# Expert products of a mixture-of-experts layer: float32 weights as the stationary operand, 21 load slots, h2 in natural column order

## The chip, the cores and the metric

The kernel runs on one core of a Trainium2 chip, in one launch. The core has TensorE (PE), VectorE (DVE), ScalarE (ACT), GpSimd (POOL) and SyncE (SP), each with its own queue of instructions, and DMA queues that are filled by SP and POOL. The metric is the device time of a launch in microseconds, lower is better.

## What is computed

One layer of a decoder for 1024 tokens of 1024 channels, all in float32: a modulated RMS norm, forgetting attention (8 heads) beside causal pooling, an output projection with residual, then a second modulated norm and a mixture of 32 small gated MLPs of which each token takes two, and a last norm. What the change touches is the second half:

```python
h = modulate(rmsnorm(x, norm_ffn_g), sh_f, sc_f)               # called h2 in the kernel
lg = h @ w_rg + b_rg                                           # 4 groups: the best one, with its probability
le_sel = (h @ w_re + b_re)[chosen group]                       # 8 experts of the group: the best two, softmax
for g in range(4):
    a = einsum('td,edf->tef', h, w_gate[g])                    # 1024 -> 256 per expert
    b = einsum('td,edf->tef', h, w_up[g])
    act = silu(a) * b * comb[:, g, :, None]                    # comb is 0 for the experts not chosen
    y = y + einsum('tef,efd->td', act, w_down[g])              # 256 -> 1024
x = rmsnorm(x + gt_f * y, norm_final_g)
```

## The kernel before

The work is tiled by 128 tokens (eight tiles) up to the router, and by expert behind it. Most of SBUF is one tile, `arena`, in which views are placed by hand at kB offsets.

**The order.** The instructions of PE, ACT, DVE and POOL are issued in the order in which the program writes them. Up to the first experts that order is `ORDER` (from line 38), a list of tokens: `om` and `oe` are the output projection of a tile and its residual, `xg` (`x1g`, line 898) multiplies x1 by the norm's factor into h2, `na` (`norm_ops`, 903) ends the norm and stores h2 with a DMA, `ro`, `rm` and `rt` transpose h2, multiply it with the router and choose, `po`, `pq` count positions, `tb` (line 1164) writes the table of each expert's tokens, `cp`, `ct`, `pc` the table of weights, `ld` is a load by SP.

**An expert.** `ex_gather` (1057) is a DMA on POOL's queue that fetches the rows of up to CAP = 100 tokens of an expert from h2 in DRAM; `ex_xt` (1080) transposes them on PE, eight transposes, and ACT and DVE copy them out of PSUM as two f16 halves. `load_chunks` (675 to 688) loads the weights, three chunks of 1 MB for an expert (gate, up, down) into the next of 14 slots of 8 kB per partition (`SLOTS`, 113); from expert 8 on a POOL memset of one element of the slot stands ahead of a load (`gate`). Since the products are made of f16 numbers, each chunk is split first: a high half (`ex_split`, by ACT, line 190 or 236) and the rest (DVE, 191, or POOL, 238). `mm3` (203 to 205) then multiplies high by high, high by low and low by high: in `ex_gu` X is the stationary operand (100 columns) and gate and up side by side are the moving one (512 columns). `ex_act` makes silu(gate) times up, `ex_at` (1103) transposes that, `ex_down` multiplies it with down, `ex_y` (1126) weighs it and `ex_scatter` (1118) adds it to x1 in DRAM by a DMA.

The experts 0 to 2 are begun in `ORDER`; the loop behind it interleaves an expert's gate and up with the down product of the one before, the transposes of the next, the splits of the next and the loads. The last two experts are kept apart and added to rows that were gathered before; `fin_load` and `fin_all` (1276 to 1304) are the last norm.

**h2's columns.** h2 is written in another column order (column 8p + j of a row lands at 128j + p), so that transposing contiguous pieces gives X in the order in which a weight chunk lies, eight rows of it in a partition. So `x1g` and `fin` (908) read and write with a stride.

Of the kernel before, what the change touches and what calls it, by code (L numbers as in the profile page):

```python
# [22 lines left out]
P = 128  # L23
S = 1024
D = 1024
# [11 lines left out]
GATE = 8  # L37
# [54 lines left out]
ld.6 oe51 pq40 av371 rt46 om600 pq41 xg51 av372 oq51 av373 bl7 om601 ho37 cm6 na50 ld.7 cm7 ld.8  # L92
ld.9 ce6 ld.10 na51 ce7 ro50 na52 ro51 na53 na54 na55 om602 om603 rm5 oe60 rt50 oq60 rt51 rt52 xg60
rt53 xs0001 rt54 xs0011 om610 om611 om612 rt55 om613 oe61 xg61 oq61 xs0101 om700 po5 na60 rt56 na61
na62 pq50 na63 pq51 om701 na64 om702 ro60 ro61 om703 om710 rm6 xs0111 na65 rt60 oe70 oq70 xg70 rt61
rt62 rt63 rt64 rt65 om711 om712 om713 oe71 xs0201 rt66 xm1 oq71 xg71 na70 po6 pq60 pq61 na71 gt na72
xm0 na73 na74 xs1001 ld.11 ro70 ro71 na75 xm2 ld.12 rm7 rt70 rt71 rt72 rt73 rt74 rt75 rt76 po7 pq70
pq71 tb cp xn0 xn1 xn2 xs0210 pc xs1100 ct ld.13 ld.14 xt00 ld.15 ld.16 xt01 xn3 xt10 xt11 gu00 xn4
gu01 xs1011 ld.17 ac0 xs1110 xs1200 xs1211 ld.18 ld.19 gu10 at0 xt20 xt21 xn5 xs2000 gu11 dw00 dw01
xs2100 ey0 sc0 xs2011 xs2110 ac1 xs2200 xs2210 ld.20 ld.21 ld.22  # L100
# [12 lines left out]
SLOTS = (40, 24, 96, 64, 72, 80, 88, 104, 0, 8, 16, 32, 56, 48)  # L113
# [4 lines left out]
def build(nc, tc, io, dbg=None):  # L118
# [559 lines left out]
    def load_chunks(upto, gate=False):  # L678
# [169 lines left out]
    wr_l = cview([P, KD, 36], F16)  # L848
    tl = {}
# [38 lines left out]
    def pj(ap, n):  # L888
        return ap.rearrange("t (p j) -> t p j", p=P)[:, n * 64:(n + 1) * 64]

    def jp(ap, n):
        return ap.rearrange("t (j p) -> t p j", p=P)[:, n * 64:(n + 1) * 64]

    def x1g(i, n):
# [27 lines left out]
    def route_t(i, q):  # L922
        h2 = tl[i]["h2"]
        hT(lambda j: h2[:, j * P:(j + 1) * P], q)
# [6 lines left out]

    def route_bias():
        sv = shf_b.rearrange("t (p j) -> t j p", p=P)
        for q in range(2):
            hT(lambda j: sv[:, j], q)
        pr = logit_mm()
        nc.vector.scalar_tensor_tensor(br_b, pr[:, 0:36], IWS, br_b, op0=OP.mult, op1=OP.add)
# [89 lines left out]
    def comb_table(o, r, dst):  # L1027
        pt = table(o, r.rearrange("p a b c -> p a (b c)"))
        nc.vector.tensor_reduce(dst, pt[:, 0:3 * NE].rearrange("p (a b) -> p b a", b=NE), axis=AX.X, op=OP.add)
        nc.vector.tensor_scalar(dst, dst, IWS / 4096.0, None, op0=OP.mult)  # L1030

    def b2_first():
# [3 lines left out]
        for g in range(4):  # L1036
            nc.sync.dma_start(wr_r[:, :, g * 8:(g + 1) * 8],
                              io["w_router_expert"][0, g].rearrange("(p j) e -> p j e", p=P))
        nc.sync.dma_start(wr_r[:, :, NE:], io["w_router_group"][0].rearrange("(p j) e -> p j e", p=P))
        load_chunks(1)  # L1040

    r_gh = Ring((152, 128), [KD, 2 * DE], F16)
    r_gl = Ring((144, 136), [KD, 2 * DE], F16)
    r_dnh = Ring((120, 160), [2, D], F16)
    r_dnl = Ring((124, 164), [2, D], F16)
    r_X = Ring((112, 116, 188), [D])
# [385 lines left out]
```

## Time and profile before

| | |
|---|---|
| Median of 3 runs | 909.32 us (907.1 to 912.29) |
| Span of the profiled execution | 909.4 us |
| PE busy | 734.2 us, 81% |
| DVE busy | 706.2 us, 78% |
| ACT busy | 499.5 us, 55% |
| POOL busy | 425.3 us, 47% |
| Moved by the DMA engines | 200.73 MB, mean 221 GB/s |

The shares are means over very different stages: the attention and pooling half runs to some 460 us, the router's end to 507 us, the experts to 871 us, the last norm to the end. A group of rows gives, for a line of the program, the busy time and what ended the idle time ahead of it; the rows of the timeline give single stretches. A matmul's record holds a fixed part that overlaps with the next one, so the price of one in a row of equals is the distance between their starts.

### The profile page before, as it was taken

Reading aid. Unit: us, or ns where it says so; the run is one execution under the profiler, and the core shown is the slowest. Engines: PE = TensorE matmul, PEld = TensorE weight load, DVE = VectorE, ACT = ScalarE, POOL = GpSimd, SP = SyncE. Lnnn points to the kernel's source line nnn. Section 1 sums busy time; section 2 is a strip of 40 time slices with the busy share of each in tenths; the row PEclk is TensorE's granted clock in tenths of the full one; section 3 lists DMA queues with packets and bytes.
Section 4 is the critical chain, followed back from the end, with each engine's and each line's share of the span. In section 5 each row is a group of like instructions: output and inputs, shape, how many; then the busy total and the mean of one; then the engine's idle time right before and its main releaser. Section 6 shows DMA issues by size and latency. Waiting matters only on the chain. (4 is left out here: it accounts for less than half of the span.)

```text
span 909.4 us, 13948 instructions
## 1 busy us (share of the span) xinstructions
PE 734.2 (81%) x4891; PEld 436.0 (48%) x4892; DVE 706.2 (78%) x1407; ACT 499.5 (55%) x776; POOL 425.3 (47%) x320
## 2 busy tenths in 40 slices
PE   2699999997978999889884299999887787888920
PEld 1358575343446565566642255555544454444510
DVE  4949877998785879967599569999877777777963
ACT  4455323221256354467744188898766677667750
POOL 2422501242104355367724357787756666565830
PEclk9999999998998999999997599999989899899975
DMA  8946675455875131125285669998999999999373
GB/s 288 383 167 202 199 230 144 135 160 160 223 215 163 62 114 37 71 106 174 83 328 204 196 205 309 354 327 291 328 309 307 302 321 320 309 317 303 79 281 124
DMA packets 108867, 200.73 MB, mean 221 GB/s; under 512 B 26219, under 2 KB 79075, under 8 KB 100598
## 3 DMA queue, kind: packets, MB, share of 16 engines
q1 hardware_dynamic: 97030, 181.83, 59.1%
q0 software_dynamic: 11760, 17.94, 8.5%
q8 instruction: 40, 0.66, 0.3%
q14 instruction: 37, 0.30, 0.1%
HBM read 177.27 MB, written 32.05 MB: 230 GB/s over the span
## 5 line engine op out<-in xcount | busy, mean ns | idle before, releaser
L191 DVE SCALAR_TENSOR_TENSOR arena<-arena 128x1024 f16<-128x1024 f32 (+1 forms) x168 | 215.5, 1306 | 44.6 <-ACT arena L190 39.1
L190 ACT ACTIVATE arena<-arena 128x1024 f16<-128x1024 f32 (+1 forms) x168 | 169.5, 1057 | 51.5 <-DMA arena<-in_w_expert_down 23.0
L205 PEld LDWEIGHTS <-arena 128*128 128x128 f16 (+1 forms) x912 | 100.8, 112 | 113.3 <-issue 26.7
L203 PEld LDWEIGHTS <-arena 128*128 128x128 f16 (+1 forms) x912 | 101.7, 113 | 102.0 <-ACT arena L1105 23.3
L204 PEld LDWEIGHTS <-arena 128*128 128x128 f16 (+1 forms) x912 | 101.4, 113 | 80.7 <-issue 19.6
L1118 POOL DMA_INDIRECT x_d<-arena,toki x30 | 102.0, 3399 | 78.9 <-DVE arena L1126 68.7
L238 POOL TENSOR_TENSOR arena<-arena 128x1024 f16<-128x1024 f32 x40 | 95.6, 2389 | 72.2 <-ACT arena L237 71.3
L786 POOL TENSOR_TENSOR arena<-arena 128x512 f16<-128x512 f32 (+1 forms) x72 | 83.2, 1165 | 70.2 <-ACT arena L785 34.8
L204 PE MATMUL pg<-arena 128*100 128x512 f16 x256 | 98.2, 383 | 4.4 <-DVE arena L191 4.3
L203 PE MATMUL pg<-arena 128*100 128x512 f16 x256 | 98.7, 386 | 1.3 <-ACT arena L190 1.3
L205 PE MATMUL pg<-arena 128*100 128x512 f16 x256 | 97.8, 382 | 0.0
L784 ACT ACTIVATE arena<-pst,psh_c 128x512 f32<-128x512 f32 (+1 forms) x80 | 52.4, 655 | 49.2 <-PE pst L777 24.1
L203 PE MATMUL py<-arena 128*100 128x512 f16 x128 | 53.8, 421 | 20.5 <-ACT arena L1105 20.5
L530 DVE SCALAR_TENSOR_TENSOR arena<-arena,cact 128x256 f32<-128x256 f32 x112 | 65.3, 583 | 2.4
L203 PE MATMUL pp<-arena 128*128 128x512 f16 x160 | 62.2, 389 | 4.6 <-DVE arena L654 4.6
L1057 POOL DMA_INDIRECT arena<-h_d,toki x32 | 55.6, 1738 | 16.6 <-PE pxt L1080 9.2
L204 PE MATMUL pp<-arena 128*128 128x512 f16 x160 | 62.0, 387 | 0.1
L205 PE MATMUL pp<-arena 128*128 128x512 f16 x160 | 61.9, 387 | 0.0
L208 ACT ACTIVATE arena<-arena 128x1024 f16<-128x1024 f32 (+2 forms) x34 | 29.1, 856 | 55.7 <-POOL arena L878 28.6
L622 POOL TENSOR_TENSOR arena<-arena 128x1039 f32<-128x1039 f32 (+3 forms) x10 | 22.7, 2266 | 79.1 <-issue 53.9
L205 PE MATMUL py<-arena 128*100 128x512 f16 x128 | 54.1, 423 | 1.0 <-DVE arena L1106 1.0
L731 DVE TENSOR_REDUCE mx<-psn 128x1 f32<-128x512 f32 (+3 forms) x76 | 47.1, 653 | 9.4 <-PE psn L730 7.6
(264 smaller groups left out, 1762.0 us busy)
## 6 DMA issues: line engine op xcount, KB each, us to landing
arena<-in_w_expert_gate SPq DMA_DIRECT2D x32, 1024.0 KB
arena<-in_w_expert_up SPq DMA_DIRECT2D x32, 1024.0 KB
arena<-in_w_expert_down SPq DMA_DIRECT2D x32, 1024.0 KB
arena<-in_w_ada SPq DMA_DIRECT2D x24, 1024.0 KB
arena<-in_x SPq DMA_DIRECT2D x17, 512.0 KB
arena<-in_w_in SPq DMA_DIRECT2D x12, 512.0 KB
arena<-in_w_out SPq DMA_DIRECT2D x8, 512.0 KB
x_d<-arena SPq DMA_DIRECT2D x8, 512.0 KB
```

Source lines behind the costliest of these rows:

```text
L190: nc.scalar.activation(wh, wr, AF.Copy, scale=WS)
L191: nc.vector.scalar_tensor_tensor(wl, wr, WS, wh, op0=OP.mult, op1=OP.subtract)
L203: nc.tensor.matmul(out, a_hi, b_hi, start=first, stop=False)
L204: nc.tensor.matmul(out, a_hi, b_lo, start=False, stop=False)
L205: nc.tensor.matmul(out, a_lo, b_hi, start=False, stop=last)
L238: nc.gpsimd.tensor_tensor(wl, wr, wh, op=OP.subtract)
L530: nc.vector.scalar_tensor_tensor(acc(), wa[:, k], cact[:, k:k + 1], acc(), op0=OP.mult, op1=OP.add)
L731: box[kh, h0] = lambda: nc.vector.tensor_reduce(mx[:, kh, h0:h0 + hb], ps[:, 0:hb * n].rearrange("p (a b) -> p a b", b=n), axis=AX.X, op=O ...
L784: nc.scalar.activation(p32[:, :ncols], ps[:, :ncols], AF.Exp, bias=psh_c, scale=0.125)
L786: (nc.gpsimd if b else nc.vector).tensor_tensor(pl[:, :ncols], p32[:, :ncols], ph[:, :ncols], op=OP.subtract)
L1057: nc.gpsimd.indirect_dma_start(out=Xt[0:w], out_offset=None, in_=src, in_offset=IndirectOffsetOnAxis(ap=tok_idx[0:w], axis=0), bounds_chec ...
L1118: nc.gpsimd.indirect_dma_start(out=dst, out_offset=IndirectOffsetOnAxis(ap=tok_idx[0:w], axis=0), in_=src, in_offset=None, bounds_check=S ...
```

## The change

Seven edits go together.

1. An expert's products use float32 operands. The weights as loaded are the stationary operand of gate and up, in blocks of 128x128, and X transposed (128 by 100, float32) is the moving one; the result is already transposed, so `ex_at` goes. For down the activation is the stationary operand and the raw weights the moving one. All splits of experts go, with their views.
2. `ex_gu(E, 0)` is gate now and `ex_gu(E, 1)` up, 16 matmuls each; both write one PSUM tile. `ex_act` has two parts: ACT's Silu on gate, and DVE's product.
3. `SLOTS` has 21 entries, and the memsets ahead of loads go.
4. h2 keeps its natural column order: `x1g` and `fin` are contiguous, and the transposes of X read with a stride of 8.
5. The router's weights are loaded in that order, and the norm's factor g2 is multiplied into them in `rb_piece`, after which they are split again; `route_t` transposes x1 and not h2.
6. The last tile's h2 is stored by POOL's queue, the others' by SP's.
7. `ORDER` is written anew from `cm6` on, and no expert product is in it; the loop runs over all experts, one after the other, with two buffers of X and of Y (three before).

```diff
-GATE = 8
-ld.6 oe51 pq40 av371 rt46 om600 pq41 xg51 av372 oq51 av373 bl7 om601 ho37 cm6 na50 ld.7 cm7 ld.8
+ld.6 oe51 pq40 av371 rt46 om600 pq41 xg51 av372 oq51 av373 bl7 om601 ho37 cm6 ld.7 cm7 ld.8 ld.9
...
-SLOTS = (40, 24, 96, 64, 72, 80, 88, 104, 0, 8, 16, 32, 56, 48)
+SLOTS = (40, 24, 96, 64, 72, 80, 88, 104, 0, 8, 144, 152, 16, 32, 112, 120, 128, 136, 56, 160.25, 48)
...
-            if gate:
-                nc.gpsimd.memset(v[0:1, 0, 0:1], 0.0)
...
-        nc.vector.tensor_tensor(jp(t["h2"], n), pj(t["x1"], n), pj(g2_b, n), op=OP.mult)
+        ns = slice(n * 512, (n + 1) * 512)
+        nc.vector.tensor_tensor(t["h2"][:, ns], t["x1"][:, ns], g2_b[:, ns], op=OP.mult)
...
-            nc.vector.scalar_tensor_tensor(h2.rearrange("t (j p) -> t p j", p=P), h2.rearrange("t (j p) -> t p j", p=P),
-                                           rs, shf_b.rearrange("t (p j) -> t p j", p=P), op0=OP.mult, op1=OP.add)
-            nc.sync.dma_start(h2_d[i * P:(i + 1) * P, :], h2)
+            nc.vector.scalar_tensor_tensor(h2, h2, rs, shf_b, op0=OP.mult, op1=OP.add)
+            (nc.gpsimd if i == NT - 1 else nc.sync).dma_start(h2_d[i * P:(i + 1) * P, :], h2)
...
-        h2 = tl[i]["h2"]
-        hT(lambda j: h2[:, j * P:(j + 1) * P], q)
+        x1 = tl[i]["x1"]
+        hT(lambda j: x1[:, j * P:(j + 1) * P], q)
...
+            nc.vector.tensor_tensor(wr_r, wr_r, g2_c.rearrange("p (k a) -> p k a", a=1).broadcast_to([P, KD, 36]),
+                                    op=OP.mult)
+            split_w(wr_r, wr_h, wr_l)
...
-            nc.tensor.transpose(pt[:, j, 0:w], Xt[0:w, (4 * q + j) * P:(4 * q + j + 1) * P], ident[0:w, 0:w])
-        h, l = (a[:, 4 * q:4 * q + 4, 0:w] for a in (xh, xl))
-        nc.scalar.activation(h, pt[:, :, 0:w], AF.Copy)
-        nc.vector.tensor_tensor(l, pt[:, :, 0:w], h, op=OP.subtract)
+            nc.tensor.transpose(pt[:, j, 0:w], Xv[0:w, 4 * q + j], ident[0:w, 0:w])
+        nc.scalar.activation(E["xT"][:, 4 * q:4 * q + 4, 0:w], pt[:, :, 0:w], AF.Copy)
...
-        for k in range(4 * part, 4 * part + 4):
-            mm3(E["pg"][0:w], E["xh"][:, k, 0:w], E["xl"][:, k, 0:w], E["gh"][:, k], E["gl"][:, k], k == 0, k == KD - 1)
+        for c in range(2):
+            for k in range(KD):
+                nc.tensor.matmul(E["pg"][:, 2 * part + c, 0:w], E["raw"](part)[:, k, c * P:(c + 1) * P],
+                                 E["xT"][:, k, 0:w], start=k == 0, stop=k == KD - 1)
...
+        if part == 0:
+            E["act"] = r_act.next()
+            nc.scalar.activation(E["act"][:, :, 0:w], E["pg"][:, 0:2, 0:w], AF.Silu)
+        else:
+            nc.vector.tensor_tensor(E["act"][:, :, 0:w], E["act"][:, :, 0:w], E["pg"][:, 2:4, 0:w], op=OP.mult)
...
-            mm3(py, ath[:, j], atl[:, j], E["dh"][:, j, ns], E["dl"][:, j, ns], j == 0, j == 1)
+            nc.tensor.matmul(py, E["act"][:, j, 0:E["w"]], E["raw"](2)[:, j, ns], start=j == 0, stop=j == 1)
...
-    for e in range(2, NE + 1):
+    for e in range(NE):
+        E = EX[e]
+        n = ORD[e]
+        ex_gu(E, 0)
+        ex_act(E, 0)
+        ex_gu(E, 1)
         if e + 1 < NE:
             ex_xt(EX[e + 1], 0)
             ex_xt(EX[e + 1], 1)
+        ex_act(E, 1)
+        if e + 3 < NE:
+            ex_new(e + 3)
...
+        load_chunks(3 * e + 2 + RING)
+        ex_down(E, 0)
+        ex_down(E, 1)
+        Y = ex_y(E, cslot[:, n:n + 1], YL.get(e))
+        if e < NE - LASTN:
+            ex_add(e)
+        else:
+            nc.vector.tensor_tensor(Y, Y, E["R"], op=OP.add)
+        load_chunks(3 * e + 3 + RING)
```

What PE does around an expert's down product, before: `pa` are the two transposes of the activation, `pxt` those of the next expert's X, and every product has three matmuls, each with its load of the stationary operand.

```order
L1103 MATMUL pa<-ident,arena 128x100 [waits DVE_49]
L1103 MATMUL pa<-ident,arena 128x100
L1080 MATMUL pxt<-ident,arena 128x100 [waits DMASW4_49,PE_49]
L1080 MATMUL pxt<-ident,arena 128x100 x3
L1080 MATMUL pxt<-ident,arena 128x100 [waits PE_49]
L1080 MATMUL pxt<-ident,arena 128x100 x3
L203 LDWEIGHTS arena [waits Activation_49]
L203 MATMUL py<-arena 100x512
L204 LDWEIGHTS arena
L204 MATMUL py<-arena 100x512
```

The same place after, from the transposes to the end of the next expert's gate and up (`pg`):

```order
L1044 MATMUL pxt<-ident,arena 128x100 [waits DMASW4_49,PE_49]
L1044 MATMUL pxt<-ident,arena 128x100 x3
L1044 MATMUL pxt<-ident,arena 128x100 [waits PE_49]
L1044 MATMUL pxt<-ident,arena 128x100 x3
L1068 MATMUL py<-arena 100x512 [waits DMAHW7_49,DVE_49]
L1068 MATMUL py<-arena 100x512 x3
L1053 MATMUL pg<-arena 128x100 [waits DMAHW1_49,Activation_49]
L1053 MATMUL pg<-arena 128x100 x3
L1053 MATMUL pg<-arena 128x100 [waits Activation_49]
L1053 MATMUL pg<-arena 128x100 x11
L1053 MATMUL pg<-arena 128x100 [waits DMAHW4_49,Activation_49]
L1053 MATMUL pg<-arena 128x100 x15
```

The down product follows the transposes directly and has four matmuls; gate is the first sixteen `pg`, up the last sixteen, and the first of up waits for ACT (for the Silu that reads gate's half of the same PSUM tile) and for its load.

The first expert on PE, before:

```order
L1080 MATMUL pxt<-ident,arena 128x100 [waits DMASW1_49,Pool_49]
L1080 MATMUL pxt<-ident,arena 128x100 x7
L1080 MATMUL pxt<-ident,arena 128x100 [waits DMASW2_49,DVE_49]
L1080 MATMUL pxt<-ident,arena 128x100 x3
L1080 MATMUL pxt<-ident,arena 128x100 [waits DVE_49]
L1080 MATMUL pxt<-ident,arena 128x100 x3
L203 LDWEIGHTS arena [waits Activation_49]
L203 MATMUL pg<-arena 100x512
```

And after:

```order
L1044 MATMUL pxt<-ident,arena 128x100 [waits DMAHW3_49,DMASW1_49]
L1044 MATMUL pxt<-ident,arena 128x100 x7
L1053 MATMUL pg<-arena 128x100 [waits Activation_49]
L1053 MATMUL pg<-arena 128x100 x3
L1053 MATMUL pg<-arena 128x100 [waits Activation_49]
L1053 MATMUL pg<-arena 128x100 x11
```

Of the two sets of transposes ahead of the first product, the one of expert 1, which waits for the second gather, has moved behind it.

POOL ahead of the first gathers, before (L238 are subtractions of splits, L1057 is the gather):

```order
L238 TENSOR_TENSOR arena<-arena 128x4x256 [waits Activation_49]
L238 TENSOR_TENSOR arena<-arena 128x4x256 [waits PE_49,Activation_49]
L238 TENSOR_TENSOR arena<-arena 128x1024 [waits DMAHW4_49,PE_49,Activation_49]
L1253 MEMSET arena 128x1024 [waits PE_49]
L1255 DMA arena<-mod_d 128x1024 [waits DMAHW4_49,DMAHW2_49,DMAHW5_49,DMAHW1_49,DMAHW7_49,DVE_49,Activation_49]
L1253 MEMSET arena 128x1024
L238 TENSOR_TENSOR arena<-arena 128x4x256 [waits DMAHW7_49,Activation_49]
L1253 MEMSET arena 128x1024 [waits DMAHW6_49,DMAHW0_49,DMAHW7_49,DVE_49,PE_49]
L1057 DMA arena<-h_d,toki 100x1024 [waits DVE_49,Pool_49]
```

And after, where L780 belongs to attention, L899 is the last tile's store of h2 and L1032 the gather:

```order
L780 TENSOR_TENSOR arena<-arena 128x512 [waits PE_49,Activation_49,Pool_49] x3
L780 TENSOR_TENSOR arena<-arena 128x384 [waits PE_49,Activation_49,Pool_49]
L899 DMA h_d<-arena 128x1024 [waits DVE_49]
L1032 DMA arena<-h_d,toki 100x1024 [waits DMAHW2_49,DMAHW3_49,DMAHW1_49,DMAHW4_49,DMAHW0_49,DMAHW6_49,DMASW0_49,DVE_49]
L1032 DMA arena<-h_d,toki 100x1024 [waits DMAHW5_49]
```

The subtractions and memsets are gone from POOL, and the store of h2 stands ahead of the gathers there.

## Rows read from the trace of the kernel before

**Rows 1.** Stretches: window, us; busy us of PE, PEld, DVE, ACT, POOL; clock; DMA; GB/s

```profile
459.00:507.00 48.00, 27.51 (x205) 15.10 (x203) 45.50 (x139) 22.58 (x39) 16.34 (x10) 0.78 0.68 255
547.00:600.00 53.00, 50.27 (x256) 29.03 (x254) 51.59 (x63) 45.48 (x60) 41.23 (x17) 1.00 1.02 333
620.00:832.00 212.00, 176.75 (x837) 100.66 (x836) 165.06 (x202) 150.10 (x200) 134.72 (x110) 0.94 0.96 312
```

**Rows 2.** Timeline of SP (start, length in us): loads 47 and 95

```profile
641.22 0.38 SPq L686 DMA_DIRECT2D arena<-in_w_expert_down  x1
...
832.47 0.38 SPq L686 DMA_DIRECT2D arena<-in_w_expert_down  x1
```

**Rows 3.** Timeline and tile view (ns min/median/max) of float32 products, modc and pada

```profile
57.63 0.81 PE L353 MATMUL modc<-ones_c,arena 128*128 128x1 f32 x6
...
L353 PEld LDWEIGHTS modc<-ones_c,arena x64: 188/192/338, 13.6 to 58.2; 128*128 128x128 f32 x64
L353 PE MATMUL modc<-ones_c,arena x64: 166/250/373, 13.6 to 58.2; 128*128 128x1 f32 x64
...
93.07 1.02 PE L494 MATMUL pada<-arena,ones_c 128*1 128x256 f32 x4
```

**Rows 4.** Timeline and tile view of float32 transposes: strided pht, contiguous pxt

```profile
282.12 0.50 PE L918 MATMUL pht<-ident,arena 128*128 128x128 f32 x3
282.24 0.19 PEld L918 LDWEIGHTS pht<-ident,arena 128*128 128x128 f32 x1
L918 PE MATMUL pht<-ident,arena x72: 270/273/445, 282.0 to 495.8; 128*128 128x128 f32 x72
581.43 0.85 PE L1080 MATMUL pxt<-ident,arena 100*128 100x100 f32 x8
...
L1080 PEld LDWEIGHTS pxt<-ident,arena x256: 138/141/230, 513.4 to 851.6; 100*128 100x128 f32 x128
```

**Rows 5.** Timeline of the last expert: a hop from PE over ACT to PE

```profile
867.57 0.39 PE L1103 MATMUL pa<-ident,arena 100*128 100x100 f32 x2 [0.93 <-DVE arena L1096]
...
868.00 0.34 ACT L1105 ACTIVATE arena<-pa 128x200 f16<-128x200 f32 x1 [0.94 <-PE pa L1103]
...
868.39 0.42 PE L203 MATMUL py<-arena 128*100 128x512 f16 x1 [0.43 <-ACT arena L1105]
```

**Rows 6.** Timeline of DVE, POOL and PE from the last norms to the first expert

```profile
469.86 2.12 DVE L981 TENSOR_TENSOR M<-arena 128x32 f16<-128x32 f16 x1
...
490.99 2.12 POOL L238 TENSOR_TENSOR arena<-arena 128x1024 f16<-128x1024 f32 x1 [8.26 <-ACT arena L237]
...
495.82 2.80 DVE L226 SCALAR_TENSOR_TENSOR r_z<-r_a,r_z 128x1 f32<-128x1 f32 x1
500.24 1.95 DVE L908 SCALAR_TENSOR_TENSOR arena<-arena,r_z 128x1024 f32<-128x1024 f32 x1
506.66 0.19 DVE L1164 TENSOR_SCALAR toki<-ptab 128x32 int32<-128x32 f32 x1 [0.30 <-PE pcn L1171]
507.84 1.57 POOL L1057 DMA_INDIRECT arena<-h_d,toki  x1 [1.56 <-DVE cb L199]
509.71 1.95 POOL L1057 DMA_INDIRECT arena<-h_d,toki  x1 [0.30 <-issue]
513.41 1.56 PE L1080 MATMUL pxt<-ident,arena 100*128 100x100 f32 x8 [2.33 <-DMA arena<-h_d,toki]
521.93 1.56 PE L1080 MATMUL pxt<-ident,arena 100*128 100x100 f32 x8 [6.96 <-DMA arena<-h_d,toki]
523.29 0.63 PE L203 MATMUL pg<-arena 128*100 128x512 f16 x1
...
540.83 1.23 DVE L191 SCALAR_TENSOR_TENSOR arena<-arena 128x1024 f16<-128x1024 f32 x1 [0.17 <-ACT arena L190]
```

**Rows 7.** Timeline of DVE at the end: the last Y, and the last norm

```profile
871.22 0.75 DVE L1126 SCALAR_TENSOR_TENSOR arena<-py,cslot,arena 100x512 f32<-100x512 f32 x1 [0.54 <-PE py L205]
...
890.21 4.87 DVE L1300 SCALAR_TENSOR_TENSOR arena<-arena 128x1024 f32<-128x1024 f32 x4
```

More of the change, by code (lines that the diff above doesn't have):

```diff
@@ L676, in build, with load_chunks @@
     nload = [0]
-    def load_chunks(upto, gate=False):
+    def load_chunks(upto):
         while nload[0] < min(upto, 3 * NE):
@@ L848, in build @@
     wr_l = cview([P, KD, 36], F16)
+    g2_c = const.tile([P, KD], F32, name="g2_c")
     tl = {}
@@ L930, in logit_mm @@
         return pr
[L932 to L937, printed above, removed]
     def route_mm(i):
@@ L1060, in ex_gather @@
         return Xt
-    def ex_split(E, w, part, f=split_w):
-        ks = slice(4 * part, 4 * part + 4)
-        if w < 2:
-            if w == 0 and part == 0:
-                E["gh"], E["gl"] = r_gh.next(), r_gl.next()
-            fs_ = slice(w * DE, (w + 1) * DE)
-            f(E["raw"](w)[:, ks], E["gh"][:, ks, fs_], E["gl"][:, ks, fs_])
-        else:
-            if part == 0:
-                E["dh"], E["dl"] = r_dnh.next(), r_dnl.next()
-            f(E["raw"](2)[:, part], E["dh"][:, part], E["dl"][:, part])
@@ L1092, in ex_act @@
-    def ex_act(E):
-        w = E["w"]
-        act = r_act.next()[0:w]
-        nc.scalar.activation(act, E["pg"][0:w, 0:DE], AF.Silu, scale=IWS)
-        nc.vector.scalar_tensor_tensor(act, E["pg"][0:w, DE:], IWS, act, op0=OP.mult, op1=OP.mult)
-        E["act"] = act
-    def ex_at(E):
-        w = E["w"]
-        pa = bank("pa").rearrange("p (a b) -> p a b", b=P)
-        for j in range(2):
-            nc.tensor.transpose(pa[:, j, 0:w], E["act"][:, j * P:(j + 1) * P], ident[0:w, 0:w])
-        ath, atl = r_ath.next()[:, :, 0:w], r_atl.next()[:, :, 0:w]
-        nc.scalar.activation(ath, pa[:, 0:2, 0:w], AF.Copy)
-        nc.vector.tensor_tensor(atl, pa[:, 0:2, 0:w], ath, op=OP.subtract)
-        E["at"] = (ath, atl)
+        for c in range(2):
+            for k in range(KD):
+                nc.tensor.matmul(E["pg"][:, 2 * part + c, 0:w], E["raw"](part)[:, k, c * P:(c + 1) * P],
+                                 E["xT"][:, k, 0:w], start=k == 0, stop=k == KD - 1)
@@ L1109, in ex_down, with ex_act @@
+    def ex_act(E, part):
+        w = E["w"]
+        if part == 0:
[3 more added lines that the diff above has]
+            nc.vector.tensor_tensor(E["act"][:, :, 0:w], E["act"][:, :, 0:w], E["pg"][:, 2:4, 0:w], op=OP.mult)
     def ex_down(E, n):
-        ath, atl = E["at"]
         ns = slice(n * 512, (n + 1) * 512)
@@ L1129, in build @@
     EX = {}
-    PARTS = [(0, 0), (1, 0), (0, 1), (1, 1), (2, 0), (2, 1)]
     def ex_raw(e):
@@ L1138, in ex_new @@
         EX[e]["X"] = ex_gather(toki[:, ORD[e]:ORD[e] + 1], CAP, r_X.next())
-    def sp_parts(e, parts):
-        if e < NE:
-            for w, p in parts:
-                ex_split(EX[e], w, p, split_p if (w, p) == (2, 1) else split_w)
     opl = {}
@@ L1384, in build @@
             with tc.For_i(1, nb, 1) as b:
-                g, u, d = (view(kb, sh) for kb, sh in ((fo[4], [KD, DE]), (fo[5], [KD, DE]), (fo[6], [2, D])))
+                g, u, d = (view(kb, sh) for kb, sh in ((fo[13], [KD, DE]), (fo[14], [KD, DE]), (fo[15], [2, D])))
                 nc.sync.dma_start(g, wg_d[ds(e, 1)].rearrange("a p j f -> (a p) j f"))
@@ L1393, in build @@
                 E = dict(w=P, raw=lambda w, t=(g, u, d): t[w], X=ex_gather(ti, P, r_X.v[0]))
-                for w, p in PARTS:
-                    ex_split(E, w, p)
                 ex_xt(E, 0)
```

95 lines of the change are left out of this document (26 added, 69 removed).

## The prediction

> **What bounds the kernel now.** I read the expert stage first, because the change rewrites it. The busy time by stretch [rows 1] shows two limits there. From 547 to 600 us DVE is busy 51.59 of 53.00 us and PE 50.27, so the engines that split float32 into halves and multiply the halves set the pace. From 620 to 832 us every engine has slack (PE 176.75 of 212) and the DMA share is 0.96: the transfers set it. Loads 47 and 95 are issued at 641.22 and 832.47 us [rows 2], 48 loads of 1 MB in 191.25 us, 3.98 us each, so 11.95 us for an expert's three. A reader should keep this pair: the old loop would take less than 11.95 us per expert if weights lay ready, because in the engine-bound stretch it does not wait for them.
>
> Then the way into the stage. Between 459 and 507 us DVE is busy 45.50 of 48 us [rows 1]: it ends the last tiles' norm and routing. The token table is written at 506.66, the first gather issued at 507.84, expert 0's transposes start at 513.41, expert 1's at 521.93, and only then the first expert matmul, 523.29 [rows 6].
>
> The profiled span is 909.4 us and the median of the runs 909.32, so I sum against the span and add nothing.
>
> **The change, part by part.**
>
> *The matmuls of an expert.* Removed: all splits on ACT, DVE and POOL, the two transposes of the activation, and three f16 products for each matmul. Added: 32 float32 matmuls for gate and up (weights stationary, 128x128; X moving, 100 columns) and 4 for down (activation stationary, 512 weight columns moving). The trace has float32 matmuls of both kinds.
>
> Each one appears as two records. Four pada records with 256 moving columns take 1.02 us, the last of them 0.38 [rows 3]: (1.02 - 0.38)/3 = 0.213 us per record. A record of 512 columns then takes twice that, 0.427; down has 4 x 2 of them, 3.42 us.
>
> For gate and up the nearest rows are modc: a contiguous float32 weight block of 128 columns is stationary, one column moves. Six records take 0.81 us, one 0.25: (0.81 - 0.25)/5 = 0.112 each [rows 3]. With one moving column the weight load must set this, and the load is slow: 192 ns, against 141 ns for the same block where it is transposed [rows 3, 4]. What a moving pass of 100 columns costs is seen in pxt: eight records in 0.85 us, about 0.086 each [rows 4]. So if load and pass overlap, a record costs the larger, 0.112; if not, 0.112 + 0.083 = 0.195. That they overlap is seen in the strided pht transposes: loads of 0.19 us beside a pass of 128 columns, three records in 0.50, (0.50 - 0.273)/2 = 0.113 each [rows 4]. I take 0.112: 32 x 2 x 0.112 = 7.17 us.
>
> The Trainium skill ("TensorE: Matmul & The Clock Gate", section "Part 3: Packing small matmuls — row/col tiling") says that weight loads overlap with running matmuls only where they use another row group of the array. By that rule each of the 64 records would pay load and pass; pht and pxt speak against it, since their loads and passes use the whole array and still cost only the longer. The same page ("Weight-path perf modes — Fast Weight Load (FWL) and DoubleRow") says that float32 weights are not loaded in the fast way, which agrees with the 192 ns of modc and speaks against a cheaper record.
>
> The transposes of X read with a stride of 8 now, as the strided pht did: 8 x 0.113 = 0.90 us.
>
> *The wait for Silu.* Gate and up share one PSUM tile, and in the order of the changed kernel the first up matmul waits for ACT, whose Silu reads the gate half. PE then has nothing else in its queue; behind it stand the next expert's transposes and down. Its price is that of the existing hop from PE over ACT to PE [rows 5]: two transposes start at 867.57 and end at 867.96, so the second, 0.25 long, starts at 867.71; ACT runs 868.00 to 868.34; PE starts again at 868.39. That is 0.68 us after the second transpose's start, where without a wait it would be 0.09: 0.59 lost. Silu may take a little longer than that copy, so I take 0.62, between 0.5 and 0.7. The DVE product after the up matmuls (200 columns; one of 512 from PSUM takes 0.75 us, [rows 7]) lies beside 0.90 us of transposes; I count nothing, and 0.8 if that cover were gone, as it is for the last expert.
>
> Per expert: 7.17 + 0.90 + 3.42 + 0.62 = **12.1 us on PE**, where it was 11.95 by transfers and 9.5 by engines.
>
> *Loads.* Bytes are the same. A raw slot is held until its matmuls have run, with 21 slots instead of 14, so loads lead by seven experts. At 3.98 us the 75 loads after the first 21 need 299 us and would end near 810 us if slots allowed, long before PE. So transfers stop being the bound, and the memsets on POOL that held loads back cost nothing either way.
>
> *The way in.* Six DVE instructions in 459 to 507 us run long while a POOL subtraction of the splits (such as the one at 490.99) runs: the first is 32 columns wide and takes 2.12 us, the last has one column and takes 2.80, longer than the 1.95 of one with 1024 columns [rows 6]. Each held against others of its line, the six lose 10.9 us. These subtractions go. Writing h2 with stride costs 1.95 us against 1.23 for a contiguous operation of that width [rows 6]; three of them give 2.2 us. So DVE could be 13.1 us earlier at the token table. PE and DVE alternate over the last tiles' output projection and routing, which the change also interleaves anew, so I take 9 (7 to 13.1). The router multiplies g2 into its weights once and early; nothing waits on that.
>
> The first matmul no longer waits for expert 1's transposes: 521.93 - 513.41 = 8.5 us. But the last tile's h2 store is on POOL's queue now, ahead of the gathers, and expert loads fill the DMA beside it: the first gather took 5.6 us (507.84 to 513.41), the second, issued at 509.71, over 11 [rows 6]. I charge 4 (0 to 6). First expert matmul: 523.3 - 9 - 8.5 + 4 = **510** (500 to 514). PE starts there at half speed as now (0.63 us for the first record [rows 6], where one of that size takes 0.42 at 868.39 [rows 5]): 2 us.
>
> *Tail.* The last Y is written from 871.22, the end is 909.4 [rows 7]: 38.8 us from the last down matmul. What follows, groups of rows with four 4.87 us operations on DVE, stays; the last addition moves from POOL (2.12 for 1024 columns) to DVE (1.23) [rows 6]: 37.9 (35 to 39).
>
> **Sum:** 510 + 2 + 31 x 12.1 + 12.0 (the last expert without transposes, with the DVE product uncovered) + 37.9 = **937 us**, 28 above the span.
>
> **Rivals.**
>
> *Loads and passes do not overlap* (the page's rule). 64 x 0.083 = 5.3 us more per expert, 170 in all: 1107 us. For it: no row here has a float32 product with both a wide load and a wide pass. Against: pht, pxt. Chance 0.06.
>
> *Faster: the record costs only its pass.* If what modc shows is the cost of a single moving column and not of the load, a record costs 0.086 as in pxt, and an expert 64 x 0.026 = 1.7 us less: period 10.45, 937 - 53 = 884 us. Loads, done by 810, would let it. It decides from a period of 11.4 us: 510 + 2 + 32 x 11.4 + 37.9 = 914, the limit of "not slower". For it: moving passes are what bounds every other stage of PE. Against: 192 ns for modc's loads against 141. Chance 0.10, with the cases between.
>
> *The clock falls.* From 620 to 832 us the granted clock is 0.94 on the mean, from 547 to 600 it is 1.00 [rows 1]; the first has PE waiting, the second nearly full. The new loop leaves one gap of 0.6 us per expert, so I expect 1.00. At 0.94: 375 x 0.06/0.94 = 24 more, 961 us. Chance 0.09.
>
> *The loop is transfer-bound after all*, because stores, gathers and loads together still take 11.95 us: hidden behind 12.1 by the lead; it would change nothing.
>
> **How the numbers follow.** The forecast's case has 0.75, and its own ends are 922 (first matmul at 500, Silu hop 0.5) and 955 (514, and a period 0.3 longer where an evacuation or bank is late). The faster rival has 0.10, of which 0.08 lies below 905 and 0.02 within the limits of no change. 0.5% is 4.5 us, about what a measurement of this kernel can tell from no change. Slower: 0.75 + 0.06 + 0.09, less 0.01 of the forecast's case that may end within them = 0.89; same 0.03; faster 0.08. The range: the forecast's case and the slower clock hold 0.84, so 918 to 964 leaves out the faster case and the non-overlapping one.
>
> **What would show it.** In the profile of the changed kernel: gate and up records 0.112 apart, down records 0.43; a gap of about 0.6 us before the first up matmul of each expert, ended by ACT; 12.1 us from one expert's first gate matmul to the next; the first at about 510; expert loads done more than 50 us before the last expert; PE over 0.95 busy at a clock of 1.00. Wrong: records 0.195 or 0.086 apart, waits of PE for weights, or a first matmul after 514.

## The result, and the profile after

The changed kernel takes 942.32 us (median of 4 runs, 940.14 to 943.3) against 908.21 us before (906.25 to 912.29): a ratio of 1.035, 95% interval 1.031 to 1.040. The forecast was 937 us in a range of 918 to 964. Slower was forecast, and slower it is.

The profiled execution has a span of 940.8 us. First the stretches of the expert stage; the columns are those of [rows 1].

```profile
497.00:512.00 15.00, 2.40 (x34) 1.94 (x33) 5.24 (x27) 0.00 (x0) 2.84 (x3) 0.50 1.02 383
512.00:600.00 88.00, 82.34 (x561) 68.31 (x562) 11.55 (x19) 10.87 (x24) 17.25 (x13) 0.95 0.86 269
600.00:700.00 100.00, 96.59 (x650) 76.70 (x648) 15.66 (x25) 10.68 (x25) 22.58 (x17) 1.00 0.98 307
700.00:800.00 100.00, 96.59 (x671) 78.62 (x670) 15.66 (x25) 10.30 (x24) 23.07 (x17) 1.00 0.98 303
800.00:900.00 100.00, 96.16 (x665) 78.03 (x665) 16.15 (x26) 13.03 (x30) 19.87 (x15) 1.00 0.51 144
```

Against [rows 1] the limits have changed places. DVE and ACT, busy 0.78 and 0.71 of the time between 620 and 832 us before, fall to 0.16 and 0.11. PE is busy 96.59 of 100 us at a granted clock of 1.00 (the share of full speed at which TensorE was let run). The row to look at is the last: from 800 to 900 us the DMA share falls to 0.51, because the loads end, and PE's figure does not move (from 835 us on, with the loads done, PE is busy 0.96 of the time at a DMA share of 0.35). A reader who sees only 600 to 800 us, with a DMA share of 0.98 beside a PE at 0.97, could take either for the limit; the stretch after the last load tells them apart. That last load is issued here, 11 us earlier than in [rows 2], though the kernel ends 31 us later:

```profile
821.11 0.38 SPq L680 DMA_DIRECT2D arena<-in_w_expert_down  x1
```

One expert on PE, in the timeline (start, length, both in us; in brackets the idle time ahead and what ended it):

```profile
642.74 0.39 PE L1053 MATMUL pg<-arena 128*128 128x100 f32 x2
643.55 3.81 PE L1053 MATMUL pg<-arena 128*128 128x100 f32 x32 [0.43 <-ACT arena L1060]
647.20 1.04 PE L1044 MATMUL pxt<-ident,arena 100*128 100x100 f32 x8
648.08 3.60 PE L1068 MATMUL py<-arena 128*100 128x512 f32 x8
651.51 3.71 PE L1053 MATMUL pg<-arena 128*128 128x100 f32 x32
655.65 0.58 PE L1053 MATMUL pg<-arena 128*128 128x100 f32 x3 [0.43 <-ACT arena L1060]
```

Up starts at 643.55 in one expert and at 655.65 in the next: a period of 12.10 us, the same for all experts but the first. The 32 up records (two for each matmul) and those of gate stand 0.112 us apart. Down's eight take 3.60 us, so (3.60 - 0.59)/7 = 0.43 each, 0.59 being the length of one. The only idle time is the bracket ahead of up, ended by ACT: the Silu.

The loads of the weights into the array answer to modc in [rows 3]; the tile view gives ns min/median/max:

```profile
L1053 PEld LDWEIGHTS pg<-arena x2048: 186/192/338, 516.2 to 901.1; 128*128 128x128 f32 x187
```

They have the 192 ns of modc, and not the 141 ns of the transposes in [rows 4].

The way in, on DVE, POOL and PE, to be held against [rows 6]:

```profile
494.80 0.84 POOL L899 DMA_DIRECT2D h_d<-arena  x1 [37.93 <-DVE lg L944]
498.79 0.19 DVE L1114 TENSOR_SCALAR toki<-ptab 128x32 int32<-128x32 f32 x1 [0.30 <-PE pcn L1121]
504.82 1.15 POOL L1032 DMA_INDIRECT arena<-h_d,toki  x1 [9.18 <-DMA arena<-in_w_expert_down]
514.67 1.60 PE L1044 MATMUL pxt<-ident,arena 100*128 100x100 f32 x8 [11.48 <-DMA arena<-h_d,toki]
516.20 5.92 PE L1053 MATMUL pg<-arena 128*128 128x100 f32 x32
```

The token table is written 7.9 us earlier than before, the first expert matmul starts 7.1 us earlier. In between, the gather is issued 6.0 us after the token table (1.2 before) and expert 0's transposes, which read its rows, start 9.8 us after that (5.6 before). The timeline puts the first delay down to a load of weights; the DMA view (512 KB, us from issue to landing) shows the store of h2 itself:

```profile
h_d<-arena POOLq DMA_DIRECT2D x1, 512.0 KB, 9.0
```

Issued at 494.80, it landed at 503.85, and the gather, which reads what it stores, starts 0.97 us behind that. The same 0.97 us stands between the two in five of the experiments below (0.86 with longer gathers), so the gather waited for the store. Whether the store and the gather are slow by themselves or by the loads beside them, the experiments had to say.

### The profile page after: what moved, and what is told of

It is laid out like the page before. It is cut to its first block, busy times and chain, and to the rows that moved or that the text cites. A ratio compares the mean times of both kernels' runs of the same rounds, so it can differ in the third digit from the quotient of the medians.

```text
span 940.8 us, 15347 instructions
## 1 busy us (share of the span) xinstructions
PE 805.2 (86%) x5979; PEld 564.5 (60%) x5980; DVE 465.2 (49%) x1161; ACT 268.9 (29%) x515; POOL 257.2 (27%) x223
## 5 line engine op out<-in xcount | busy, mean ns | idle before, releaser
L1053 PEld LDWEIGHTS pg<-arena 128*128 128x128 f32 x2048 | 238.1, 193 | 34.8 <-ACT arena L1060 19.0
L1053 PE MATMUL pg<-arena 128*128 128x100 f32 x2048 | 243.0, 277 | 13.6 <-ACT arena L1060 13.6
L1062 DVE TENSOR_TENSOR arena<-arena,pg 128x200 f32<-128x200 f32 x32 | 11.6, 361 | 241.8 <-PE pg L1053 241.8
L1068 PE MATMUL py<-arena 128*100 128x512 f32 x256 | 115.2, 593 | 0.5 <-DVE arena L1062 0.5
L780 POOL TENSOR_TENSOR arena<-arena 128x512 f16<-128x512 f32 (+1 forms) x72 | 80.6, 1130 | 70.2 <-ACT arena L779 35.3
L1080 DVE SCALAR_TENSOR_TENSOR arena<-py,cslot,arena 100x512 f32<-100x512 f32 x64 | 48.1, 752 | 100.0 <-PE py L1068 100.0
L1032 POOL DMA_INDIRECT arena<-h_d,toki x32 | 34.8, 1087 | 203.1 <-PE pxt L1044 193.6
L201 PEld LDWEIGHTS <-arena 128*128 128x128 f16 x528 | 50.8, 99 | 58.1 <-issue 14.9
L199 PEld LDWEIGHTS <-arena 128*128 128x128 f16 x528 | 51.6, 100 | 45.3 <-issue 12.7
L200 PEld LDWEIGHTS <-arena 128*128 128x128 f16 x528 | 51.0, 99 | 43.1 <-issue 11.4
L1045 ACT ACTIVATE arena<-pxt 128x400 f32<-128x400 f32 x64 | 30.5, 503 | 155.7 <-PE pxt L1044 155.5
L1072 POOL DMA_INDIRECT x_d<-arena,toki x30 | 48.0, 1601 | 94.8 <-DVE arena L1080 91.6
L1068 PEld LDWEIGHTS py<-arena 128*100 128x100 f32 x256 | 41.0, 170 | 51.1 <-issue 50.4
L779 ACT ACTIVATE arena<-pst,psh_c 128x512 f16<-128x512 f32 (+1 forms) x80 | 52.4, 655 | 0.0
L201 PE MATMUL pso<-arena 128*128 128x512 f16 x128 | 50.5, 395 | 0.0
```

Of the source, the lines that this page charges most:

```text
L199: nc.tensor.matmul(out, a_hi, b_hi, start=first, stop=False)
L200: nc.tensor.matmul(out, a_hi, b_lo, start=False, stop=False)
L201: nc.tensor.matmul(out, a_lo, b_hi, start=False, stop=last)
L779: nc.scalar.activation(ph[:, :ncols], ps[:, :ncols], AF.Exp, bias=psh_c, scale=0.125)
L780: (nc.gpsimd if b else nc.vector).tensor_tensor(pl[:, :ncols], p32[:, :ncols], ph[:, :ncols], op=OP.subtract)
L1053: nc.tensor.matmul(E["pg"][:, 2 * part + c, 0:w], E["raw"](part)[:, k, c * P:(c + 1) * P], E["xT"][:, k, 0:w], start=k == 0, stop=k == KD - 1)
```

## The experiments

The theory after the result: PE alone sets the pace of the stage, by records of 0.112 us whose length the load of the weights into the array sets, with the Silu wait on top; the start is late because loads of weights stand beside the store of h2 and the first gather. The rivals: the transfers are just behind PE, so that nothing can be won by a quicker PE; the records follow the moving pass; the store and the gather are slow by themselves.

### The Silu wait taken away

```diff
-        if part == 0:
-            E["pg"] = bank2("pg").rearrange("p (a b) -> p a b", b=P)
+        E["pg", part] = bank2("pg").rearrange("p (a b) -> p a b", b=P)
...
```

> Gate and up of an expert write two PSUM tiles instead of one, all else as in the changed kernel. In the changed kernel's trace the first up matmul starts 0.70 us after the last gate matmul, 0.59 more than the 0.112 between others, in every expert. If PE alone sets the pace, this gap goes and nothing takes its place: 32 x 0.59 = 18.8 us, period 11.5, about 923 us. If the transfers (3 x 3.98 = 11.95 us per expert) are a second limit just behind, the period stops at 11.95 and the time at about 938 us. If the wait is hidden anyway: 942 us.

Measured: 921.93 us, ratio 1.012 (1.009 to 1.015). An expert on PE:

```profile
642.21 1.04 PE L1044 MATMUL pxt<-ident,arena 100*128 100x100 f32 x8
643.08 3.60 PE L1067 MATMUL py<-arena 128*100 128x512 f32 x8
646.52 5.72 PE L1052 MATMUL pg<-arena 128*128 128x100 f32 x50
```

No bracket is left, and the period is 11.43 us in every expert: 0.67 less, 0.59 of it the Silu hop, and 0.08 one longer spacing (0.19 us) among the up records, which is gone too. PE is busy 100.00 of 100 us from 600 to 700. A period below 11.95 shows that the transfers did not hold PE up: with 21 slots the loads ran ahead, the last issued at 807.22. The second expectation, 938 us, falls.

### Half the moving columns

```diff
-                                 E["xT"][:, k, 0:w], start=k == 0, stop=k == KD - 1)
+                                 E["xT"][:, k, 0:w // 2], start=k == 0, stop=k == KD - 1)
...
```

> The gate and up matmuls of every expert take 50 of its up to 100 token columns as moving operand and leave the other 50 out (they count as zero in what follows); stationary loads, number of matmuls and everything else stay. If the load of a float32 block of 128 columns sets a record's price, the spacing stays at 0.112 us and the time at 939 to 942 us (Silu and product a little shorter). If the moving pass sets it (100 columns in 0.083 us), or load and pass add up, the pass falls by 0.042 us in 64 records of 32 experts: 85 us less, 857 us.

Measured: 1083.91 us, ratio 1.19 (1.18 to 1.20). Neither theory had that. A stretch of the stage, and two experts on PE in its timeline:

```profile
700.00:800.00 100.00, 97.93 (x484) 77.99 (x483) 10.56 (x18) 7.58 (x18) 16.83 (x13) 0.71 0.68 227
```

```profile
703.37 3.67 PE L1053 MATMUL pg<-arena 128*128 128x50 f32 x32
707.38 6.93 PE L1053 MATMUL pg<-arena 128*128 128x50 f32 x32 [0.34 <-ACT arena L1060]
714.11 1.56 PE L1044 MATMUL pxt<-ident,arena 100*128 100x100 f32 x8
715.46 4.77 PE L1068 MATMUL py<-arena 128*100 128x512 f32 x8
720.07 3.67 PE L1053 MATMUL pg<-arena 128*128 128x50 f32 x32
```

Two things are to be seen. Where the clock is full, 32 records with 50 columns take 3.67 us, against 3.71 with 100: the spacing is still 0.112. So the moving pass does not set it, as the theory had it. But the granted clock is 0.71 on the mean, PE being as busy as ever: the next 32 records take 6.93 us, 0.21 apart, at the lower of the two levels, and in both experts shown the clock falls again. The price of a record was read rightly; that the clock would fall was not foreseen. Since the other 50 columns stand as zeros in the activation, down's stationary operand is half zeros in this run too; no run separates that from the narrower passes.

### 128 moving columns

```diff
-CAP = 100
+CAP = 128
```

> The changed kernel with 128 instead of 100 token rows per expert: moving passes of 128 columns in gate and up, the same loads of weights. If the load of 128 float32 columns (0.112 us) sets a record, and a pass of 128 columns takes 0.107, the spacing and the period stay at 0.112 and 12.1 us and only the gather and scatter grow: 941 to 946 us. If the record follows the pass, 0.028 x 0.83 = 0.023 us more in each of 64 records of 32 experts: 48 us more, 990 us. If load and pass add up in part, in between.

Measured: 939.14 us, ratio 1.031 (1.026 to 1.036).

```profile
646.12 3.73 PE L1053 MATMUL pg<-arena 128*128 128x128 f32 x32
650.32 3.84 PE L1053 MATMUL pg<-arena 128*128 128x128 f32 x32 [0.47 <-ACT arena L1060]
```

The same spacing with 128 columns as with 100 (3.73 against 3.71 for 32 records); the period is 12.21, the 0.11 more lying mostly in the longer Silu hop. With 50, 100 and 128 columns the record costs 0.112 at full clock, so it is not the pass that sets it. What is left is the weight load, always of 128 columns here. No run narrows that block, so a fixed price of 0.112 for any record of a float32 product would look the same; for the load speaks that the transposes of X stand 0.111 apart with loads of 206 ns and 0.086 with loads of 141 (next run, and [rows 4]). The time is not above that of the changed kernel because the token table was written 4.2 us earlier in the profiled run. The edit does not do that: with the same instructions ahead of it, the table came at 494.59 here, 498.79 in the changed kernel, and 501.36 and 501.53 in the two runs above, so a single trace tells the way in to some 7 us.

### X read contiguously again

```diff
-        Xv = E["X"].rearrange("t (p j) -> t j p", p=P)
+        Xv = E["X"].rearrange("t (j p) -> t j p", p=P)
...
-        nc.vector.tensor_tensor(t["h2"][:, ns], t["x1"][:, ns], g2_b[:, ns], op=OP.mult)
+        nc.vector.tensor_tensor(jp(t["h2"]), pj(t["x1"]), pj(g2_b), op=OP.mult)
...
```

> h2 is written in the old column order again (product and norm's end with a stride), so that the transposes of X read contiguously; the rest as in the changed kernel. By the prediction's terms the eight transposes fall from 0.111 to 0.086 us apart: 8 x 0.025 x 31 = 6 us less, and three to four strided DVE operations per stretch put the token table 2 to 3 us later: 938 to 940 us, first gate matmul near 518.5. If a stride costs nothing in the transposes: 944 us. If the later DVE work is hidden behind PE or the store of h2: 936 us.

Measured: 946.5 us, ratio 1.040 (1.033 to 1.047); span of the profile 942.1.

```profile
646.90 3.82 PE L1055 MATMUL pg<-arena 128*128 128x100 f32 x32 [0.43 <-ACT arena L1062]
650.55 0.85 PE L1046 MATMUL pxt<-ident,arena 100*128 100x100 f32 x8
651.24 1.96 PE L1070 MATMUL py<-arena 128*100 128x512 f32 x4
```

The eight transposes take 0.85 us instead of 1.04, as expected. The period falls only to 11.99, by 0.11: the transposes are also the cover of DVE's product, and the second record of down now starts 0.51 us after the first instead of 0.43. That it waits there for the product is likely, not shown. The token table is at 503.75 us, which the 7 us between traces of the same instructions don't let one put down to the strided operations. So the contiguous read gives back 3.4 us in the stage, and the kernel is no faster; the 938 to 940 us expected did not come.

### The loads held back from the start

```diff
...
+    def late_loads():
+        for c in range(nload[0], RING):
+            nc.vector.tensor_copy(view(SLOTS[c], [D])[0:1, 0:1], EX[0]["X"][0:1, 0:1])
+        load_chunks(RING)
```

> The loads 15 to 20, which the changed kernel issues from 487.7 to 503.2 us, are held back until the first gather has landed (DVE copies one element of the gathered rows into each of their slots). Theory: the store of the last h2 tile (issued 494.80) and the gather (504.82, landed 514.6) are slow because these loads fill the DMA engines; without them the store lands within 4 us and the gather within 5 to 6, the first gate matmul starts 8 to 10 us earlier, near 507, and the time is 933 us. Rival: the store on POOL's queue and the gather have that latency by themselves: 942 us. Second rival: the loads are then late for the experts 5 and 6 and PE waits for them: above 942 us.

Measured: 934.2 us, ratio 1.024 (1.017 to 1.030).

```profile
497.08 0.84 POOL L899 DMA_DIRECT2D h_d<-arena  x1 [36.40 <-DVE lg L944]
501.05 0.19 DVE L1114 TENSOR_SCALAR toki<-ptab 128x32 int32<-128x32 f32 x1 [0.30 <-PE pcn L1121]
501.58 1.15 POOL L1032 DMA_INDIRECT arena<-h_d,toki  x1 [3.65 <-DVE cb L192]
506.97 1.60 PE L1044 MATMUL pxt<-ident,arena 100*128 100x100 f32 x8 [1.47 <-DMA arena<-h_d,toki]
508.50 6.23 PE L1053 MATMUL pg<-arena 128*128 128x100 f32 x32
```

And the store in the DMA view of this run:

```profile
h_d<-arena POOLq DMA_DIRECT2D x1, 512.0 KB, 3.2
```

From the token table to the first expert matmul it takes 7.45 us, in the changed kernel 17.41. The store still goes through POOL's queue, but it lands 3.2 us after its issue instead of 9.0, ahead of the token table; the gather now waits for DVE alone, and its rows are there 5.4 us after its issue. So the 10 us belonged to the loads beside them: in all runs that keep the 21 slots filled from the start the distance is 15.4 to 18.2 us, in all three that hold the loads back 7.4 to 7.6. The six loads are issued from 507.12 to 510.37 instead, and no expert waits for them.

### 16 slots instead of 21

```diff
...
-SLOTS = (40, 24, 96, 64, 72, 80, 88, 104, 0, 8, 144, 152, 16, 32, 112, 120, 128, 136, 56, 160.25, 48)
+SLOTS = (40, 24, 96, 64, 72, 80, 88, 104, 0, 8, 144, 152, 16, 32, 112, 120)
```

> The changed kernel with 16 load slots instead of 21 (the loads 16 to 20 go into the loop). If PE alone sets the pace, 12.1 us per expert against 11.95 us of transfers, five slots less cost nothing in the stage, and the period stays 12.10; at the start fewer loads stand beside the store of h2 and the first gather, which held back cost 9.8 us in the run with late loads, so 4 to 8 us less: 934 to 938 us. If the lead of seven experts is needed, PE waits for weights at some experts and the time is 946 us or more.

Measured: 933.54 us, ratio 1.025 (1.018 to 1.032). The period is 12.10 in every expert but the first, and the first matmul starts 8.7 us after the token table. Fewer slots are not worse but better, since the five loads that are missing were those that stood beside the gather.

### Down in f16 again, gate and up in float32

```diff
...
+    def ex_dsplit(E):
+        E["dh"], E["dl"] = r_wdh.next(), r_wdl.next()
+        for j in range(2):
+            split_w(E["raw"](2)[:, j], E["dh"][:, j], E["dl"][:, j])
...
-            nc.tensor.matmul(py, E["act"][:, j, 0:E["w"]], E["raw"](2)[:, j, ns], start=j == 0, stop=j == 1)
+            mm3(py, h[:, j], l[:, j], E["dh"][:, j, ns], E["dl"][:, j, ns], j == 0, j == 1)
...
```

> Only the down product goes back to three f16 products, its weights split by ACT and DVE (busy 11 and 16 per cent of the stage now), gate and up stay float32; the order on PE is gate, down of the expert before, transposes, up, so that no wait of Silu is left, and two slots go to the halves (19). PE-bound theory: 7.17 + 0.89 + 12 x 0.2157 = 10.65 us per expert instead of 12.10, 31 x 1.45 = 45 us less: 897 us, faster than the kernel of before. If transfers are the next limit at 11.95, or the loads fall behind: 937 us. If PE's granted clock falls, as it did with 50 moving columns (0.70 on the mean): above 950 us.

Measured: 888.83 us, ratio 0.976 (0.973 to 0.980).

> The kernel with f16 down products, and the loads from 15 on held back until the first gather has landed. If both effects are on the path that sets the end, they add up: 9.8 us less than the kernel with f16 down products, 887 us. If the transfers are near the limit there (77 loads of 3.98 us from 507 end near 815 us, PE's last expert starts near 840), nothing or less is gained: 890 to 897 us.

Measured: 885.89 us, ratio 0.973 (0.969 to 0.976), below both kernels. An expert of this one on PE, and two stretches:

```profile
641.24 1.03 PE L1048 MATMUL pxt<-ident,arena 100*128 100x100 f32 x8
642.11 7.31 PE L1057 MATMUL pg<-arena 128*128 128x100 f32 x64
649.25 0.38 PE L199 MATMUL py<-arena 128*100 128x512 f16 x1
...
651.63 0.38 PE L201 MATMUL py<-arena 128*100 128x512 f16 x1
651.84 0.36 PE L1048 MATMUL pxt<-ident,arena 100*128 100x100 f32 x2
```

```profile
600.00:700.00 100.00, 100.00 (x799) 90.76 (x799) 41.95 (x56) 33.04 (x57) 26.87 (x20) 1.00 0.98 320
700.00:800.00 100.00, 100.00 (x789) 89.78 (x789) 44.57 (x58) 33.93 (x57) 24.17 (x18) 1.00 0.98 322
```

The period is 10.60 us, 1.50 less than in the changed kernel, and PE has no gap. Two things give that: 0.67 is the wait for Silu, which the new order avoids, and 0.83 is down, as the distance to the 11.43 us of the run without that wait shows. DVE rises from 0.16 to 0.43, ACT from 0.11 to 0.33: engines that the change had emptied take the splits of one chunk in three. Holding the loads back moved the first expert matmul to 7.6 us after the token table (13.1 in the kernel without it, which has two slots and so two loads fewer at the start). The two medians lie 2.9 us apart, the spans 6.7, the profiled run of the kernel without it being the slowest of its five; 9.8 would have been the full effect, of which the two loads fewer had taken a part already.

The transfers have not become quicker, though. Two gate loads of this kernel, those of the experts 16 and 30:

```profile
614.65 1.24 SPq L680 DMA_DIRECT2D arena<-in_w_expert_gate  x1
783.10 0.33 SPq L680 DMA_DIRECT2D arena<-in_w_expert_gate  x1
```

That is 12.03 us for each of the 14 experts between them, where PE takes 10.60, with a DMA share of 0.98. The loads lose 1.4 us per expert against PE, and the lead with which they began hides it to the end of the stage. With many more experts, by these figures, the transfers would set the pace again.

### Both repairs with all products in float32

> The changed kernel with both repairs that leave every expert product in float32: two PSUM tiles (922 us) and late loads (9.8 us at the start). If they add up: 912 us, no difference from the kernel before, with 11.43 us per expert, below the 11.95 that the transfers took before. If the transfers become the limit at that pace, after a later start of the loads: 916 to 920 us.

The two edits are those shown above.

Measured: 912.22 us, ratio 1.000 (0.997 to 1.003). They add up: against the kernel before the changed one has 1.035, the first repair takes 0.024 off that, the second 0.012, both together 0.035. And they give no more than the kernel before: without any wait and without the late start, 64 records of gate and up, 8 of down and 8 strided transposes are 7.12 + 3.44 + 0.88 = 11.43 us per expert (the period measured; the terms are rounded).

### Natural column order in the kernel before

```diff
-            nc.vector.scalar_tensor_tensor(h2.rearrange("t (j p) -> t p j", p=P), h2.rearrange("t (j p) -> t p j", p=P),
-                                           rs, shf_b.rearrange("t (p j) -> t p j", p=P), op0=OP.mult, op1=OP.add)
+            nc.vector.scalar_tensor_tensor(h2, h2, rs, shf_b, op0=OP.mult, op1=OP.add)
...
```

> The kernel before with one part of the change alone: h2 in natural column order, the norm's factor in the router's weights, strided transposes of X; order, splits and 14 slots as before. By the prediction's terms DVE has 2 to 3 us less ahead of the token table, and the eight transposes of an expert 0.2 us more. If the stage is bound by transfers, both disappear in it: the loads are paced by the slots, and the time falls by at most the 2 to 3 us of an earlier start: 906 to 909 us against 909. If the earlier start is passed on in full, or the routing without a wait on h2 gives more: 900 to 904 us. If the strided transposes count: 911 to 915 us.

Measured: 912.64 us, ratio 1.003 (1.000 to 1.006). This kernel does not compute the layer: with the router on x1 in the old order of instructions its result is another one. Why was not followed up; the experts chosen, and so the counts of tokens, may differ, and the time decides little. The next run leaves the router on h2.

> The kernel before with h2 in natural column order alone: the router still reads h2, its weights are as before but for the order in which they are loaded. DVE has 2 to 3 us less to do before the token table, the transposes of an expert take 0.2 us more. If the transfers set the end, the first is swallowed by the loads, whose pace does not change, and the time is 908 to 912 us. If the earlier way in counts in full: 906 us or less. If the strided reads of X cost in the stage, 32 x 0.2 = 6 us: 915 us.

Measured: 905.42 us, ratio 0.991 (0.988 to 0.994).

```profile
503.07 0.19 DVE L1163 TENSOR_SCALAR toki<-ptab 128x32 int32<-128x32 f32 x1 [0.30 <-PE pcn L1170]
519.52 0.63 PE L203 MATMUL pg<-arena 128*100 128x512 f16 x1
828.51 0.38 SPq L686 DMA_DIRECT2D arena<-in_w_expert_down  x1
```

Against [rows 2] and [rows 6] the token table is 3.6 us earlier, the first expert matmul 3.8, the last load 4.0, the end 5.2 (span 904.2). The earlier start goes through the stage: loads 18 to 36 are each issued 4.1 us earlier than in the kernel before, the later ones 2.5 to 4.2. The expectation that the loads swallow it was wrong. The reading that fits is that a load waits for its slot and the slot for the matmuls, so that the stream of loads starts earlier when the experts do. That the order of h2 is what brought the token table forward is not shown by one trace: in the run before this one, with the same order of h2 (and the router's edits), it came at 508.52, later than in the kernel before.

## Why the prediction was right

Step by step, as the prediction put them.

**Gate and up, 0.112 us per record: right.** It is 0.112 at 50, 100 and 128 moving columns. The choice between the prices 0.086 and 0.112 carried the sign of the result; it was made by modc's 192 ns load [rows 3], and the loads of gate and up show the same 192. Load and pass overlap, since the spacing does not move with the pass. So the sentence of the Trainium skill ("TensorE: Matmul & The Clock Gate", section "Part 3: Packing small matmuls — row/col tiling") that they do so only for different row groups does not hold for these full-array products; the same section also lets a load into the background weight buffer go ahead, a case that the prediction left out.

**Down 0.427 and transposes 0.113: right**, 0.43 and 0.111 measured. The transposes were right with some luck: the price came from pht with 128 moving columns, and contiguous pht records in the same trace stand 0.109 apart too, so that row could not show what a stride costs. The contiguous run above does, 0.086 against 0.111 at 100 columns.

**The Silu wait 0.62: right**, 0.59 by the trace; taking it away, with the smaller gap, gave 20 us of the 942.

**The period 12.1: right** to the last digit shown, 12.10.

**The first expert matmul at 510: wrong by 6.2 us** (516.20). The step that failed is the term for the contention of the gather and of the h2 store with the loads, taken as 4 us of 0 to 6. By the prediction's own sum 8.1 us lie between token table and first matmul, to which the term is added; 17.41 were measured, so the term is 9.3, and the run with late loads, at 7.45, would make it 10.0. The rest of the miss is the token table, forecast for 497.7, 498.79 in this trace and up to 501.5 in others of the same instructions, so that this term's hit is in part luck. What was overlooked is that the store and the gather stand in line, each paying: the store took 9.0 us instead of 3.2 and the gather 9.8 instead of 5.4, and the gather did not start before the store had landed.

**The half clock at the start 2 us: right**; the first period is 14.31, 2.2 over the others.

**The tail 37.9: too long.** The last down record starts at 905.07 and the span ends at 940.8, 35.7 us. The same distance was 38.6 before (the prediction read 38.8). With the last expert, 11.6 us instead of 12.0, it comes with the opposite sign, and so the sum hid 2.6 of the 6.4 us that the start and its slow first period missed: 937 against a span of 940.8. The prediction's range has a slip as well: the terms that it names for the upper end of its own case add up to some 951 and not 955, which the result does not hang on.

**Transfers are no longer the bound: right** for these 32 experts. The period went to 11.43 and 10.60 when PE was relieved, and the DMA share fell to 0.51 in the stretch with the last loads while PE kept its pace. But in the quickest kernel the loads still come 12.0 us apart for an expert (the gate loads at 614.65 and 783.10 above), so it is the lead of the loads that takes them off the path, as the prediction's last rival had it.

**The rivals.** That load and pass add up (1107 us) and that the record costs only its pass (884 us) both fell with the spacing. The clock rival (961 us) did not happen in this kernel, 1.00 from 600 us on; in the run with half the columns it did, 0.71. The loads as the cause of a late start were in the sum; as a rival they had deserved their own range.

Where the expected gain of the change went is then plain. From the first expert matmul to the last down record it takes 388.9 us (516.20 to 905.07), before 347.5 (523.29 to 870.80), so 41 us more; the earlier start and the shorter tail give 10 back. The kernel before ran its experts at 9.45 us each while weights lay ready (first down records of ten experts from 553.8 to 648.3) and at 12.0 on the mean behind that (17 more to 851.7), when the transfers set the pace. The change relieved DVE (0.78 to 0.16), ACT and the slots, and put 12.1 us of PE time on every expert, more than either. The form that keeps most of the relief, has no Silu wait and gives back the dearest float32 records (down, 3.43 us for four matmuls against 2.59 for twelve in f16) is faster than both.

## What to carry to other kernels

Price a float32 matmul by its records, as they stood here: two for each, each the longer of 0.112 us with a stationary block of 128 columns and a pass of 0.83 ns per moving column (0.213 us for 256 [rows 3], 0.43 for 512). With 128 moving columns or fewer the first decided. Three f16 products were cheaper on PE than one float32 product (down 2.59 against 3.43 us; gate and up 24 matmuls 0.216 apart before, 5.2 us, against 7.1), as long as other engines had time for the splits. When one engine is emptied, add up the new sum of the engine that takes the work before counting the relief, and look whether a stretch with idle DMA keeps its pace. Prefetching beside a short transfer that everyone waits for cost the changed kernel 8 us and brought it nothing: tie the bulk loads to the landing of that transfer.

## What the runs showed of the hardware that was not expected

With the number of matmuls and loads unchanged, halving the moving columns of gate and up brought the granted clock of the stage from 1.00 to 0.71, at a busy share of PE that stayed at 0.98, and the kernel from 942 to 1084 us. With 100 and with 128 columns it was 1.00. Half of down's stationary columns were zeros in that run as well.

A float32 block of 128 columns takes 192 ns to load for a product and 141 for a transpose, both contiguous; with a stride of 8 the transposes of X have about 206 (median of the tile view, 190 to 226).

Under a DMA share of 1.02 the store of one 512 KB tile and a gather of 100 rows took 9.0 and 9.8 us from issue to landing; with the bulk loads held back, 3.2 and 5.4.
